# LRU and query products on VectorE, spread x loads, six query tiles, and whole-column expert loads summed in eight shared banks

## The chip, the core and the metric

The kernel runs on one core of a Trainium2 chip. The metric is the device time of one execution in microseconds (us). The core has a matrix engine, TensorE (PE in the profile, with PEld for its weight loads), VectorE (DVE), ScalarE (ACT), GpSimd (POOL) and SyncE (SP, which only issues transfers). Each engine works through its own list of instructions in order and waits where an operand is not ready. SP, ACT and POOL issue DMA transfers. Matrix products accumulate in eight banks of 128 x 512 f32, called `b` in the profile.

## What is computed

One layer of a decoder over 256 tokens of width 2048, with two sub-layers and a modulation (`mod`, from the vector c through `w_ada`):

```python
shift1, scale1, gate1, shift2, scale2, gate2 = split(silu(c) @ w_ada + b_ada, 6)
h = rms_norm(x, norm1_g) * (1 + scale1) + shift1
proj = h @ w_in
lru_out = gelu(lru_gate) * rg_lru(causal_conv(lru_x))     # a recurrence h_t = a_t h_{t-1} + b_t
ssd_out = mamba2_heads(z, xbc, dt)                        # chunked state-space scan
x = x + gate1 * (concat(lru_out, ssd_out) @ w_out)
h2 = rms_norm(x, norm2_g) * (1 + scale2) + shift2
q = h2 @ w_q                                  # 8 heads, product keys, top 16 of 128^2 experts
act = gelu(<h2, u_tab[e]>);  out = sum_k gate_k * act_k * v_tab[e_k]
return rms_norm(x + gate2 * out, final_norm_g)
```

The tables `u_tab` and `v_tab` have 16384 rows of 2048 f32 (134 MB each).

## The kernel before, in words

**Products in two halves.** All large products are f32 made of two parts in the TensorE format: hi = the rounded value, lo = the rest; a product is hi*hi + hi*lo + lo*hi. Weights stream through one pipeline in units of 128 x 1024 f32 (0.5 MB). A unit is loaded into a `raw` buffer (four of them, `NRAW`), ScalarE writes its hi half into an `hl` buffer (L144), VectorE the lo half (L153), TensorE uses it. There are four `hl` buffers (`NHL`), so ScalarE's split of unit n + 4 waits until TensorE is done with unit n. A new load is issued right after a unit's lo, which frees its `raw` buffer. `take` hands a unit to the products, `issue_split` orders the next split, `issue_lo` the lo that lags two splits behind.

**The order.** It is written out by hand: the program emits instructions slot by slot, and side work is put between the slots by `defer` (runs some slots later), `bg_pop` and `bg_flush` (a list of background steps) and `mid` (runs what was deferred). A slot is one unit's products.

**The stages.** Modulation and the first norm (0 to 150 us); input projection with the SSD scan beside it (150 to 434) and the LRU blocks (434 to 555); output projection (555 to 774), whose second half of modulation rows is summed on VectorE: `ada_step` (L384) adds one 128 x 1024 tile of `w_ada`, loaded into one of two `adr` buffers, times a column; the rates `ADA_SSD`, `ADA_LRU`, `ADA_OUT` say how many such steps go with a slot, 96 in all. Then h2 and the query (774 on), then the expert scores.

**LRU.** In `lru_scan` POOL forms gx*m (L694) ahead of the scan, in `lru_out` t*h (L709) behind it, each 128 x 1024, for four blocks.

**h2 and the query.** h2 is made in 16 parts. `h2_t` multiplies x by the inverse norm (VectorE L959, or POOL L957 for odd parts above 2), ScalarE adds the shift and makes hi (L971, or L966 and L967), VectorE makes lo (L969, L973). All parts are ordered ahead of the query products; the loop over four quarters of the columns then takes two units each, for `NQ` = 4 query tiles of 128 outputs (L1211 to L1213), and the other 12 tiles go one by one through `tile_h2` (L444, L446: one 512-wide and one 256-wide matmul per column block).

**Experts.** 80 of the 128 columns of experts (a column is 128 experts) are sparse: all scores are computed (`u_quad`, to 1357 us) and written to memory (`ad`), the chosen ones' weights are gathered back (`w_gather`, L1332, POOL) with the chosen rows of v (`v_gather`, L1323, POOL), and `v_quad` (L1353) sums four tokens at a time: 64 quads, each 32 matmuls. `w_make` prepares a quad's weights: a gelu on ScalarE (L1339), then a product on VectorE into `Wz` (L1343). The other 48 columns (`JD`) are dense: `u_slot` scores all tokens against a column (two half slots per column, 1357 to 1741 us), then `v_slot` (L1439) sums weights times v, twelve matmuls a slot. `wsplit` (L437 on ScalarE, L438 on VectorE) splits one column's weights into hi and lo. `tick` runs after every slot of both dense stretches: it lets the `late` list run (the `w_make` of the next quad) and calls `sparse` when a quad is due.

**Banks and merges.** Quads use banks 0 to 3 for the first 128 tokens and then again for the second; V slots use the other four for the first 1024 output columns over all 48 expert columns, then again for the other 1024. So each set is emptied twice by `merge` (L1461 multiplies by gate 2, L1463 adds to the rows), and the 16 merges lie after quad 31, at the switch of V halves, and at the end. `final` (L1472 to L1483) normalises 128 tokens and stores them.

## Time and profile before

| | |
|---|---|
| median of three runs | 2157.16 us (2155.39 to 2159.13) |
| the profiled execution | 2172.81 us, span 2171.1, mean granted TensorE clock 0.986 |
| TensorE busy | 2089.6 us, 96% of the span, 13092 matmuls |
| VectorE, ScalarE, GpSimd busy | 1397.3, 960.7, 879.2 us |
| moved by DMA | 616.33 MB, mean 284 GB/s |

The profile is of one execution, on one core. Rows of a timeline read: start, length, engine, line, operation, output<-inputs, shapes, count, and in brackets the idle time before with what ended it. The chain of waits follows the last instruction back to what released it, step by step. Groups read: line, engine, operation, shapes, count | busy us, mean ns | idle before and what ended it. "Granted clock" is the share of full speed that TensorE got. Line numbers of the profile of before are those of the listing above; in the changed kernel they are some 5 to 30 higher (L144, L153, L444, L446 become L149, L158, L449, L451; L1353 becomes L1374; L1439, L1450; L437, L442; L1339, L1356; L1343, L1360; L1461 and L1463, L1476 and L1478).

### The profile page before, as it was taken

How to read it: one execution, taken by the hardware profiler on the slowest of the kernel's cores; microseconds unless marked ns; L12 is line 12 of the kernel's file. 1: busy time of each engine (PE TensorE's matmuls, PEld its weight loads, DVE VectorE, ACT ScalarE, POOL GpSimd, SP SyncE). 2: the span in 40 equal slices, each digit the busy share in tenths (PEclk: the TensorE clock that was granted, in tenths of full speed). 3: DMA queues.
4: the chain of work that ended last, by engine and by line, in shares of the span. 5: the costliest groups of instructions: out<-in, count | busy, mean ns of one | idle time of the engine just before them, and what ended most of it. 6: DMA issues, size and time to landing. Idle time of an engine off the chain costs nothing.

```text
span 2171.1 us, 34830 instructions
## 1 busy us (share of the span) xinstructions
PE 2089.6 (96%) x13092; PEld 1639.8 (76%) x13092; DVE 1397.3 (64%) x1996; ACT 960.7 (44%) x1470; POOL 879.2 (40%) x729
## 2 busy tenths in 40 slices
PE   7999999999999989999999999999999989999996
PEld 4779999978999888888788778666666656656663
DVE  2368887978878868879979996334334344344344
ACT  3346665666644454444345554333333333333332
POOL 0013233312212010001415561677777757767774
PEclk9999999999999999999999999999999999999998
DMA  9966566767789954568677778799999999999996
GB/s 372 387 233 223 195 207 216 235 224 251 262 295 322 334 176 166 191 220 282 229 255 238 247 247 288 270 367 346 347 343 354 347 325 346 373 345 348 358 356 234
DMA packets 248264, 616.33 MB, mean 284 GB/s; under 512 B 37752, under 2 KB 121864, under 8 KB 225800
## 3 DMA queue, kind: packets, MB, share of 16 engines
q1 hardware_dynamic: 188944, 387.73, 51.9%
q0 software_dynamic: 45056, 175.52, 21.9%
q10 hardware_dynamic: 14096, 50.86, 6.9%
q8 instruction: 103, 1.69, 0.3%
q14 instruction: 65, 0.53, 0.1%
HBM read 692.41 MB, written 14.69 MB: 326 GB/s over the span
## 4 chain that ended last, share of the span: by engine, by line
PE 70%; DVE 14%; DMA 9%; issue 4%; ACT 2%; POOL 0%; SPq 0%; another core or an unknown queue 0%; DVEq 0%; POOLq 0%; ACTq 0%
PE b L444 13%; PE b L1439 12%; PE b L1353 10%; PE b L446 7%; DVE hl L153 6%; PE b L1281 3%; PE b L1279 3%; PE b L1280 3%; PE b L918 3%; DMA raw<-in_w_in 2%; DMA two<-in_w_ada 2%; DMA adw<-in_w_ada 2%; PE b L812 2%; PE b L813 2%; PE b L814 2%
## 5 line engine op out<-in xcount | busy, mean ns | idle before, releaser
L144 ACT ACTIVATE hl<-raw 128x1024 fp32r<-128x1024 f32 x594 | 628.6, 1060 | 1072.2 <-PE b L1439 192.7
L153 DVE TENSOR_TENSOR hl<-raw,hl 128x1024 fp32r<-128x1024 f32 x594 | 766.5, 1301 | 140.2 <-ACT hl L144 121.0
L444 PE MATMUL b<-H,hl 128*128 128x512 f32 x1376 | 494.2, 402 | 3.2 <-DVE qT L450 2.8
L446 PE MATMUL b<-H,hl 128*128 128x256 f32 x1376 | 386.6, 281 | 5.2 <-DVE hl L153 5.1
L444 PEld LDWEIGHTS b<-H,hl 128*128 128x128 f32 x1376 | 259.1, 188 | 89.9 <-issue 20.2
L1332 POOL DMA_INDIRECT X<-ad,X x256 | 289.5, 1131 | 87.9 <-issue 76.8
L1439 PE MATMUL b<-hl,X 128*128 128x512 f32 x1152 | 279.0, 400 | 11.8 <-issue 10.0
L1439 PEld LDWEIGHTS b<-hl,X 128*128 128x128 f32 x1152 | 216.6, 191 | 87.0 <-issue 39.4
L446 PEld LDWEIGHTS b<-H,hl 128*128 128x128 f32 x1376 | 260.5, 189 | 7.4 <-DVE hl L153 6.6
L1281 PE MATMUL b<-hl,H 128*128 128x512 f32 x640 | 249.9, 390 | 4.0 <-DVE hl L153 3.7
L1279 PE MATMUL b<-hl,H 128*128 128x512 f32 x640 | 252.7, 395 | 0.0
L1280 PE MATMUL b<-hl,H 128*128 128x512 f32 x640 | 249.4, 390 | 0.0
L1323 POOL DMA_INDIRECT vq<-in_v_t,X x128 | 151.5, 1184 | 114.5 <-PE b L1353 38.1
L1323 POOL DMA_INDIRECT tk<-in_v_t,X x128 | 144.0, 1125 | 71.2 <-PE b L1353 31.4
L814 PE MATMUL b<-H,hl 128*128 128x256 f32 x560 | 160.0, 286 | 4.2 <-DVE hl L153 4.2
L1343 DVE TENSOR_TENSOR Wz<-X 128x4 f32<-128x4 f32 x64 | 11.0, 172 | 236.3 <-DMA X<-ad,X 123.0
L812 PE MATMUL b<-H,hl 128*128 128x256 f32 x560 | 162.4, 290 | 0.0
L813 PE MATMUL b<-H,hl 128*128 128x256 f32 x560 | 159.7, 285 | 0.0
L1281 PEld LDWEIGHTS b<-hl,H 128*128 128x128 f32 x640 | 120.1, 188 | 31.7 <-DVE hl L153 6.8
L384 DVE SCALAR_TENSOR_TENSOR adacc<-adr,cact,adacc 128x1024 f32<-128x1024 f32 x90 | 127.7, 1419 | 21.9 <-DMA adr<-in_w_ada 21.8
L1279 PEld LDWEIGHTS b<-hl,H 128*128 128x128 f32 x640 | 120.1, 188 | 23.9
L1280 PEld LDWEIGHTS b<-hl,H 128*128 128x128 f32 x640 | 120.3, 188 | 23.7
(323 smaller groups left out, 3212.2 us busy)
## 6 DMA issues: line engine op xcount, KB each, us to landing
raw<-in_u_t SPq DMA_DIRECT2D x208, 512.0 KB
raw<-in_w_in SPq DMA_DIRECT2D x146, 512.0 KB
adr<-in_w_ada SPq DMA_DIRECT2D x96, 512.0 KB
adw<-in_w_ada SPq DMA_DIRECT2D x64, 512.0 KB
raw<-in_w_o SPq DMA_DIRECT2D x64, 512.0 KB
raw<-in_u_t ACTq DMA_DIRECT2D x48, 512.0 KB
raw<-in_v_t SPq DMA_DIRECT2D x48, 512.0 KB
raw<-in_v_t ACTq DMA_DIRECT2D x48, 512.0 KB
```

Source lines behind the costliest of these rows:

```text
L144: act.activation(t[:, 0], r, AF.Copy)
L153: dve.tensor_sub(t[:, 1], r, t[:, 0].bitcast(FT))
L444: pe.matmul(ps, w[:, 0, c], x[:, k].rearrange("p a b -> p (a b)"), start=(k == 0), stop=False, skip_group_check=True)
L446: pe.matmul(ps[:, :256], w[:, 1, c], x[:, k, 0], start=False, stop=(k == 15), skip_group_check=True)
L812: pe.matmul(ps, wh, hT[:, k, 0, :], start=(k == 0), stop=False)
L1279: pe.matmul(o, hh, w[:, 0, :, kk], start=(k == 0), stop=False)
L1280: pe.matmul(o, hl_, w[:, 0, :, kk], start=False, stop=False)
L1281: pe.matmul(o, hh, w[:, 1, :, kk], start=False, stop=(k == 15))
L1323: pool.indirect_dma_start(x, None, vf, bass.IndirectOffsetOnAxis(ap=eV[:, t:t + 1], axis=0), bounds_check=E1 - 1, oob_is_err=False)
L1332: pool.indirect_dma_start(wA[:, n:n + 1], None, adf, bass.IndirectOffsetOnAxis(ap=eW[:, t:t + 1], axis=0), bounds_check=T * E1 - 1, oob_is ...
L1353: pe.matmul(sb[c][32 * g:32 * g + 32, :], Wz[:, x:x + 32], vs[4 * (q % 2) + g][:, c * 512:(c + 1) * 512], start=(m == 0), stop=(m == 31), ...
L1439: pe.matmul(ob[tb * 2 + c], w[:, i, s], v[:, k, c * 512:(c + 1) * 512], start=(jj == 0 and (i, k) == (0, 0)), stop=(jj == JD - 1 and k == 1))
```

## The change

- **Rates.** `ADA_SSD` .65 to .80, `ADA_LRU` 1.1 to .85, `ADA_OUT` .74 to .80; the number of steps stays 96.
- **POOL to VectorE.** The LRU's two products, and the odd parts of `h2_t`.
- **x loads.** The four loads of x for the second sub-layer's residual go behind output slots 16, 19, 22 and 25 instead of all behind slot 15.
- **Query.** `NQ` = 6. The making of h2 and the query products alternate by quarters: four parts of h2, their products, three splits. In the first quarter the two row copies of x (L855) follow the splits; in the later ones each unit's products stand together.
- **Dense loads.** U and V columns are loaded whole (128 x 2048, 1 MB), alternately from SP and ACT, each into two neighbouring slots of one `raw` tile. V goes column by column, both halves of a column in a row, and `wsplit` runs once per column, the first two in the U slots of columns `JD - 4` and `JD - 3`, the others one column ahead.
- **Shared banks.** `row_bank` gives each (128 tokens, 512 columns) one bank, into which quads and V slots both sum. The merges are left for the end, eight of them.
- **Quads.** The pace is 63 quads over 188 ticks instead of 62 over 192.
- **End.** The last two columns are held back: first 128 tokens of both, quad 61 between, the first four merges, quad 62, then the second 128 tokens, `final(0)`, quad 63, four merges, `final(1)`.

```diff
-ADA_SSD, ADA_LRU, ADA_OUT = 0.65, 1.1, 0.74
+ADA_SSD, ADA_LRU, ADA_OUT = 0.8, 0.85, 0.8
-NQ = 4
+NQ = 6
...
-    items.extend(u_t[J1 + jj][:, h * 1024:(h + 1) * 1024] for jj in range(JD) for h in range(2))
-    items.extend(v_t[J1 + jj][:, h * 1024:(h + 1) * 1024] for h in range(2) for jj in range(JD))
+    items.extend(u_t[J1 + jj] for jj in range(JD))
+    items.extend(v_t[J1 + jj] for jj in range(JD))
...
+    raw = wp.tile([128, NRAW, 1024], FT, name="raw")
     def issue_dma():
...
+        while st["item"] < len(items):
+            n = st["item"]
+            a, w = st["dma"], 1 + (n >= n_alt)
+            if a + w - NRAW > st["lo"]:
+                break
+            o = raw[:, a % NRAW:a % NRAW + w].rearrange("p n c -> p (n c)")
...
-                pool.tensor_tensor(gx, gx, m, op=OP.mult)
+                dve.tensor_tensor(gx, gx, m, op=OP.mult)
...
-            pool.tensor_tensor(t, t, LR["h"], op=OP.mult)
+            dve.tensor_tensor(t, t, LR["h"], op=OP.mult)
...
-            for i in range(4):
-                x_load(i)
+        if n in (16, 19, 22, 25):
+            x_load((n - 16) // 3)
...
-                pool.tensor_tensor(t, x2[k // 4][:, k % 4], rstd2, op=OP.mult)
+                dve.tensor_tensor(t, x2[k // 4][:, k % 4], rstd2, op=OP.mult)
...
+    for q in range(4):
+        w = [take() for _ in range(NQ // 2)] if q == 0 else []
+        for k in range(4 * q, 4 * q + 4):
+            h2_part(k)
+            for e in range(0 if q else NQ):
+                q_mm(w[e // 2], k, e)
+        if q == 0:
+            for _ in range(NQ // 2):
+                issue_split()
+            for f in last:
+                f[1]()
+            continue
+        for n in range(NQ // 2):
+            w = take()
+            for k in range(4 * q, 4 * q + 4):
+                for e in (2 * n, 2 * n + 1):
+                    q_mm(w, k, e)
+            issue_split()
...
+    def row_bank(tb, c):
+        if (tb, c) in sb:
+            return sb[tb, c], False
+        sb[tb, c] = bank(4 * tb + c)
+        return sb[tb, c], True
...
-        if n >= 6 and sq["n"] < 62 * (n - 3) // (4 * JD - 4):
+        if n >= 6 and sq["n"] < 63 * (n - 3) // (4 * JD - 4):
...
-    def v_slot(h, jj):
...
-        if (h, jj) not in Wl:
+    def v_slot(jj, h):
+        if h == 0 and vst["q"] <= jj + 1:
             wsplit()
-        wsplit()
...
-        R[tb, c] = R.get((tb, c), 0) + 1
-        if R[tb, c] == 2:
-            act.activation(ps, a, AF.Square, accum_out=rf[:, tb, c:c + 1])
+        act.activation(ps, a, AF.Square, accum_out=rf[:, tb, c:c + 1])
...
         u_slot(jj)
+        if jj in (JD - 4, JD - 3):
+            wsplit()
...
+    vl = [(jj, h, take()) for jj in (JD - 2, JD - 1) for h in range(2)]
+    issue_lo(0)
+    mid()
+    for tb in range(2):
+        for n, (jj, h, v) in enumerate(vl):
+            v_part(jj, h, tb, v)
+            if tb == 0 and h == 1:
+                if n == 3:
+                    for c in range(4):
+                        merge(0, c, sb[0, c])
+                while late:
+                    late.pop(0)()
+                sparse()
```

How the rows stand, at three places. The first is ScalarE where the query begins: `rstd` is the inverse norm, `H<-adr` and `adr<-adr` make parts of h2 (`H`), `xrow` are the row copies, `hl<-raw` are splits of coming units. Before, its last rows ahead of the splits:

```order
L971 ACTIVATE H<-adr,mod 128x256
L966 ACTIVATE adr<-adr,mod 128x256
L967 ACTIVATE H<-adr 128x256
L855 ACTIVATE xrow<-b_7688 128x512
L855 ACTIVATE xrow<-b_7693 128x512
L144 ACTIVATE hl<-raw 128x1024 x9
```

With the change, from the norm on:

```order
L951 ACTIVATE rstd_7485<-b_6624,epsc 128x256
L975 ACTIVATE H<-adr,mod 128x256 x3
L971 ACTIVATE adr<-adr,mod 128x256
L972 ACTIVATE H<-adr 128x256
L149 ACTIVATE hl<-raw 128x1024 x3
L860 ACTIVATE xrow<-b_7472 128x512
L860 ACTIVATE xrow<-b_7477 128x512
L975 ACTIVATE H<-adr,mod 128x256
L971 ACTIVATE adr<-adr,mod 128x256
```

Part 4 of h2 (the last L975 row) has moved behind three splits and the row copies; the same happens, without the copies, ahead of parts 8 and 12.

The second place is ScalarE at the step from U to V: `xt` is a dense column's scores and their gelu, `X<-Wt` is `wsplit`, the 128 x 4 row is the gelu of a quad's gathered weights. Before:

```order
L136 DMA raw<-in_v_t 128x1024
L449 ACTIVATE xt<-b_16171 128x256
L1339 ACTIVATE X_7791<-X_7791 128x4
L144 ACTIVATE hl<-raw 128x1024
L1409 ACTIVATE xt<-xt 128x256
L449 ACTIVATE xt<-b_16258 128x256
L1409 ACTIVATE xt<-xt 128x256
L437 ACTIVATE X_16316<-Wt 128x256 x2
```

With the change, two columns earlier and at the step:

```order
L1429 ACTIVATE xt<-xt 128x256
L442 ACTIVATE X_15604<-Wt 128x256
L149 ACTIVATE hl<-raw 128x1024
L140 DMA raw<-in_v_t 128x2048
L454 ACTIVATE xt<-b_15607 128x256
L149 ACTIVATE hl<-raw 128x1024
L1429 ACTIVATE xt<-xt 128x256
L1356 ACTIVATE X_7911<-X_7911 128x4
```

The first two `wsplit` rows no longer stand behind the last columns' splits and gelus.

The third place is VectorE at the end: `Wz` is a quad's weights, `b<-b,H` and `H<-H,b` are a merge. Before, the last V slot's merges and what follows:

```order
L1343 TENSOR_TENSOR Wz<-X_7791 128x4
L438 TENSOR_TENSOR X_16316<-Wt,X_16316 128x256 x2
L1461 TENSOR_TENSOR b_17930<-b_17930,H 128x512
L1463 TENSOR_TENSOR H<-H,b_17930 128x512
...
L1343 TENSOR_TENSOR Wz<-X_7791 128x4 x2
L1472 TENSOR_TENSOR H<-H 128x512 x2
```

With the change:

```order
L1360 TENSOR_TENSOR Wz<-X_7911 128x4
L158 TENSOR_TENSOR hl<-raw,hl 128x1024
L443 TENSOR_TENSOR X_15604<-Wt,X_15604 128x256
L158 TENSOR_TENSOR hl<-raw,hl 128x1024
L1476 TENSOR_TENSOR b_12539<-b_12539,H 128x512
L1478 TENSOR_TENSOR H<-H,b_12539 128x512
...
L1360 TENSOR_TENSOR Wz<-X_7911 128x4 x2
L1485 TENSOR_TENSOR H<-H 128x512 x2
```

The weights of quads 62 and 63 stand behind four merges in both; before, the merges were of the V banks and a quad followed them at once, now they are of the first 128 tokens, and 24 more V matmuls follow quad 62.

More of the change, by code (lines that the diff above doesn't have):

```diff
@@ L334, in hybrid_kernel @@
         if n == 2:
-            for _ in range(NRAW):
-                issue_dma()
+            issue_dma()
         mid()
@@ L960, in h2_t, with h2_part @@
                                          op0=OP.mult, op1=OP.mult)
[L961 to L963 removed]
+    pq = [bank(1 + n) for n in range(NQ // 2)]
+    def h2_part(k):
         t = ht[k // 4][:, k % 4]
@@ L971, in hybrid_kernel, with q_mm @@
             act.activation(h2[:, k, 0], t, AF.Identity, bias=mod[:, 4, k:k + 1])
-            h2_t(k + 2)
             dve.scalar_tensor_tensor(h2[:, k, 1], t, mod[:, 4, k:k + 1], h2[:, k, 0].bitcast(FT),
                                      op0=OP.add, op1=OP.subtract)
-    for f in last:
-        f[1]()
+        h2_t(k + 2)
+    def q_mm(w, k, e):
+        ps = pq[e // 2][:, (e % 2) * 256:(e % 2) * 256 + 256]
+        c = slice((e % 2) * 512 + k % 4 * 128, (e % 2) * 512 + (k % 4 + 1) * 128)
+        first = k == 0 and e % 2 == 0
+        pe.matmul(ps, w[:, 0, c], h2[:, k, 0], start=first, stop=False, skip_group_check=True)
+        pe.matmul(ps, w[:, 0, c], h2[:, k, 1], start=False, stop=False, skip_group_check=True)
+        pe.matmul(ps, w[:, 1, c], h2[:, k, 0], start=False, stop=(k == 15), skip_group_check=True)
+    h2_t(0)
+    h2_t(1)
+    for q in range(4):
[16 more added lines that the diff above has]
+            issue_split()
     mixs.close()
@@ L1516, in hybrid_kernel @@
     mid()
-    for h in range(2):
-        for jj in range(JD):
-            v_slot(h, jj)
-            if h == 0 and jj in (0, JD // 2, JD - 4):
-                rows_load((0, JD // 2, JD - 4).index(jj))
+    for jj in range(JD - 2):
+        for h in range(2):
+            v_slot(jj, h)
+            if h == 0 and jj in (0, JD // 3, 2 * JD // 3):
+                rows_load((0, JD // 3, 2 * JD // 3).index(jj))
             tick()
-    while sq["n"] < 63:
-        tick()
-        sparse()
-    tick()
+    assert sq["n"] == 61
+    wsplit()
+    vl = [(jj, h, take()) for jj in (JD - 2, JD - 1) for h in range(2)]
+    issue_lo(0)
     mid()
-    mid()
+    for tb in range(2):
+        for n, (jj, h, v) in enumerate(vl):
+            v_part(jj, h, tb, v)
+            if tb == 0 and h == 1:
[5 more added lines that the diff above has]
+                sparse()
+    while late:
+        late.pop(0)()
     final(0)
```

84 lines of the change are left out of this document (28 added, 56 removed).

## Prediction

> **What bounds the kernel now.** I read the page's busy line first, then the engines stretch by stretch (columns: stretch, its length, busy time with instruction count of PE, PEld, DVE, ACT, POOL, then granted clock, DMA share, GB/s).
> ```profile
> PE 2089.6 (96%) x13092; PEld 1639.8 (76%) x13092; DVE 1397.3 (64%) x1996; ACT 960.7 (44%) x1470; POOL 879.2 (40%) x729
> 150.00:434.00 284.00, 279.16 (x2081) 259.13 (x2081) 244.41 (x340) 171.00 (x314) 91.86 (x79) 1.00 0.64 211
> 434.00:555.00 121.00, 112.73 (x724) 102.58 (x722) 95.89 (x103) 82.67 (x117) 25.34 (x14) 0.97 0.71 235
> 555.00:774.00 219.00, 212.55 (x1491) 199.29 (x1490) 175.10 (x175) 103.29 (x127) 31.91 (x21) 0.98 0.86 301
> 1357.00:1737.00 380.00, 377.49 (x2426) 254.22 (x2425) 146.55 (x214) 128.63 (x215) 285.51 (x242) 1.00 0.93 339
> 1737.00:2147.00 410.00, 395.80 (x2200) 250.15 (x2198) 168.75 (x248) 137.37 (x235) 283.55 (x260) 0.98 0.95 345
> ```
> TensorE is the bound at 96%, and the change removes no sizable TensorE work. What can be won are its holes: 8 us in the LRU stretch, 6 in the output projection, 14 in the dense V stretch, and the clock lost behind them. The dense U stretch has 2.5 us of holes in 380. Two numbers price a V stretch: three slots of twelve matmuls, and one sparse quad, at full clock.
> ```profile
> 2126.10 3.57 PE b L1353 x32
> 2129.67 8.38 PE b L1439 x36
> ```
> So a slot is 8.38/3 = 2.79 us, and a slot with its third of a quad 2.79 + 3.57/3 = 3.98.
>
> **Dense V, gains.** At the step from U to V, `wsplit` (L437) stood behind a split that waited for a transfer, and TensorE stood still (a timeline: start, length, idle before).
> ```profile
> 1744.58 1.06 ACT L144 ACTIVATE hl<-raw 128x1024 fp32r<-128x1024 f32 x1 [3.64 <-remote]
> 1747.54 5.49 PE L1439 MATMUL b<-hl,X 128*128 128x512 f32 x12 [6.41 <-issue]
> ```
> The first two `wsplit`s now come three and two U columns before the end; the V units themselves were split ahead. Gone: 6.41, and 5.49 - 2.79 = 2.70 of slow clock, together 9.1 (0 if the late transfer holds the slot anyway; three units lie ready, so I take 9.1). At the switch of halves, merges on VectorE freed the banks in pieces:
> ```profile
> 1946.81 3.01 PE L1439 MATMUL b<-hl,X 128*128 128x512 f32 x12
> 1957.89 2.35 PE L1353 MATMUL b<-tk,Wz 128*32 128x512 f32 x20
> ```
> 11.08 us for three slots instead of 8.38; there is no switch any more: 2.7. Twice the ScalarE `wsplit` stood behind a gelu that waited for gathered weights:
> ```profile
> 1898.54 0.20 ACT L1339 ACTIVATE X<-X 128x4 f32<-128x4 f32 x1 [2.85 <-DMA X<-ad,X]
> 1899.10 4.61 PE L1439 MATMUL b<-hl,X 128*128 128x512 f32 x12 [1.80 <-issue]
> 1926.70 4.61 PE L1439 MATMUL b<-hl,X 128*128 128x512 f32 x12 [1.79 <-ACT X L437]
> ```
> Each cost 1.8 + (4.61 - 2.79) = 3.6. A `wsplit` now serves two slots and runs two slots ahead, so a 2.85 us delay is covered by 5.6; but splits still queue behind the gelu. I take 5 of 7.2 (ends 0 and 7.2).
> The last two rows also tell about the clock: an idle gap of 1.8 us was followed by a slot at 4.61 instead of 2.79. [...]
>
> **Dense loads, whole columns.** 96 loads of 1 MB replace 192 of 0.5 MB, each into two of four slots, so a load is issued when both slots are free. For 0.5 MB the nearest landings and ScalarE's waits are
> ```profile
> 45.63 10.76 DMA raw<-in_w_in
> 555.96 5.06 DMA raw<-in_w_o
> ACT hl L144 <- DMA raw<-in_u_t: 84.4, 48, 4.2
> L153 DVE TENSOR_TENSOR hl<-raw,hl 128x1024 fp32r<-128x1024 f32 x594 | 766.5, 1301 | 140.2 <-ACT hl L144 121.0
> 1382.53 6.29 PE L1353 MATMUL b<-vq,Wz 128*32 128x512 f32 x32 [1.15 <-issue]
> ```
> The loop of a pair of slots is four slots of TensorE, 4 x 3.98 = 15.9; less two splits of 1.06 (the row at 1744.58) and one lo of 1.30 (L153's mean), a load may take 12.5. Twice 5.06 is 10.1, twice 10.76 is 21.5, but that one lay behind a full queue with four loads at once; here at most two are under way. I take 1.5 us of loss for single late loads (0 to 24, the first rival). [...] `wsplit` falls from 96 to 48 on ScalarE and VectorE, which idle there: nothing.
>
> **First quad.** It is gated by the gathers of its weights, and moves forward by one half slot (8 pairs of matmuls, 0.35 us each):
> ```profile
> 1362.13 1.00 POOL L1332 DMA_INDIRECT X<-ad,X  x1 [10.12 <-DMA raw<-in_u_t]
> 1367.21 0.40 PE L444 MATMUL b<-H,hl 128*128 128x512 f32 x1
> 1367.56 0.40 PE L444 MATMUL b<-H,hl 128*128 128x512 f32 x1
> 1368.91 3.64 PE L1353 MATMUL b<-tk,Wz 128*32 128x512 f32 x32 [0.84 <-issue]
> ```
> The gathers start no earlier, so TensorE waits 2.8 longer: loss 2.8 (0 to 5 with slow clock).
>
> **Output projection.** Four x loads went in at once and delayed the `w_ada` transfer, on which an accumulation (L384) and behind it a lo waited:
> ```profile
> 630.27 11.73 DMA adr<-in_w_ada
> 644.58 0.58 PE L874 MATMUL b<-ylru,hl 128*128 128x256 f32 x1 [3.76 <-DVE hl L153]
> 650.49 0.21 PE b L873
> 653.12 0.12 PE b L873
> ```
> The matmuls of the six microseconds behind it took 0.21 each where 0.12 is usual: some 3 us more. Three slots apart, I take a gain of 4.5 (1 to 7). The rate .80 adds 2.5 `w_ada` steps at 1.42 (L384's mean, below) and 1.2 MB in a stretch with DMA at .86: loss 1 (0 to 3).
>
> **LRU and SSD.** Eight products leave POOL for VectorE, four of L694 and four as large of L709.
> ```profile
> L694 POOL TENSOR_TENSOR X<-X,X 128x1024 f32<-128x1024 f32 x4 | 10.9, 2724 | 57.2 <-ACT X L693 57.2
> L384 DVE SCALAR_TENSOR_TENSOR adacc<-adr,cact,adacc 128x1024 f32<-128x1024 f32 x90 | 127.7, 1419 | 21.9 <-DMA adr<-in_w_ada 21.8
> 502.68 4.62 DVE L384 SCALAR_TENSOR_TENSOR adacc<-adr,cact,adacc 128x1024 f32<-128x1024 f32 x2
> ```
> VectorE has no such row; the nearest is L153 at 1.30, so 8 x 1.3 = 10.4 us more. Against that, beside a POOL product two accumulations took 4.62 instead of 2.84, so eight products cost VectorE up to 8 x 1.8 = 14 already, and the rate .85 takes about 7 steps of 1.42 = 10 away. VectorE comes out some 10 us lighter, of which holes and slow clock (8.3, and 0.03 x 121 = 3.6) can return 10 at most; that a product is done 1.4 sooner helps as well. I take a gain of 5 (-4 to 10: the lower end if POOL's work was hidden). In the SSD stretch 4.6 more steps load VectorE by 6.6, where it is 244 of 284 busy: loss 1.5 (0 to 4).
> [...]
>
> **Query.** TensorE's rows and ScalarE's at the place:
> ```profile
> 776.80 2.78 DVE L959 SCALAR_TENSOR_TENSOR adr<-X,mod,rstd 128x256 f32<-128x256 f32 x3
> 778.44 0.58 PE L1211 MATMUL b<-H,hl 128*128 128x256 f32 x1 [3.98 <-ACT H L971]
> 780.02 0.58 PE L1212 MATMUL b<-H,hl 128*128 128x256 f32 x1 [1.00 <-DVE H L973]
> 790.09 1.07 ACT L855 ACTIVATE xrow<-b 128x512 f32<-128x512 f32 x2
> 791.05 3.90 ACT L144 ACTIVATE hl<-raw 128x1024 fp32r<-128x1024 f32 x4
> ```
> Before, ScalarE produced all sixteen hi parts ahead of any split, so TensorE never waited after 780. Now part 4 stands behind three splits and two row copies, and the first of these splits needs the buffer that TensorE reads until its last step of the first quarter: 3 x 0.98 + 1.07 + 0.5 (a hi, taken as one of the two row copies) less 12 matmuls of 0.12 still running, 3.1, with the semaphores 3.5, plus 1.9 of slow clock: 5.4. At the second and third quarter one split (0.98) and one hi (0.5) lie behind TensorE's end, with lo and semaphores 2.1 each. Gained: without POOL's product the three rows at 776.80 need about 1.1 instead of 2.78, and the 1.00 gap shrinks by 0.6: 2.3. Two more tiles as three matmuls instead of a wide pair: 0.2. Net loss 5.4 + 4.2 - 2.3 + 0.2 = 7.5 (3 to 13).
>
> **Tail.**
> ```profile
> 2148.57 5.34 PE L1353 MATMUL b<-tk,Wz 128*32 128x512 f32 x32 [4.00 <-DVE Wz L1343]
> 2160.54 0.69 DVE H L1463
> 2161.23 0.62 DVE b L1461
> ```
> Before, quad 62 waited 4.0 for its weights, and the second half's merges stood behind the first half's finish. Now quad 62's weights (L1360) stand behind four merges (two operations each, 4 x (0.69 + 0.62) and steps between), so TensorE waits about 5.2 there, then has 24 matmuls and quad 63 to do, and the last merges follow without the finish between. Laid out row by row the end comes 1.4 earlier (-5 to 2 later).
>
> **Sum.** Gains 9.1 + 2.7 + 5 + 2 + 4.5 + 5 + 1.4 = 29.7; losses 1.5 + 2.8 + 1 + 1.5 + 7.5 = 14.3; net 15.4. The profiled execution took 2172.81 (span 2171.1), 0.7% over the median of 2157.16, with no stretch that stands out; I take 15.4 off both: 2157.4 for such an execution, 2142 for the median.
>
> **Rivals.** (1) Slower: two 1 MB loads in the ring are too few. From a landing of 12.5 us each further 1 us costs one per loop, 48 loops: at 13.0 it is 24 us, 2142 + 24 = 2166; it outweighs the gain from 12.8. For it: 84.4 us of ScalarE waits for 0.5 MB loads already, DMA at .93 to .95. Against: only 10.1 by the row at 555.96, and TensorE's 2.5 us of holes in 380. 0.11. (2) No change: the dense stretches are limited by DMA, and what TensorE wins there is given back as waits for loads; then only 4.5 + 5 + 1.4 - 1 - 1.5 - 7.5 = 0.9 is left: 2156. For it: .95. Against it this row of the page, slices of 54 us:
> ```profile
> GB/s 372 387 233 223 195 207 216 235 224 251 262 295 322 334 176 166 191 220 282 229 255 238 247 247 288 270 367 346 347 343 354 347 325 346 373 345 348 358 356 234
> ```
> 372 and 387 were reached, 345 is the V stretch. 0.12. [...] (3) The VectorE moves don't do what they say: LRU at -4 and the query at 13, 2142 + 9 + 5.5 = 2157. 0.07. The forecast, 0.70: 2124 (stalls, LRU and x loads at their upper ends, 2.2 + 5 + 5 + 2.5 more, and 3.5 less lost in the query) to 2152.
>
> The measurement tells a change from 0.2%, 4.3 us, on. Faster: the forecast and a little of rival 3, 0.72; same: rival 2 and most of 3, 0.15; slower: rival 1 and a worse tail or query, 0.13. Range 2124 to 2160: it leaves out rival 1's long end and the best sums.
>
> **What would show it.** No idle before the first V slot, none in mid V; TensorE holes of some 3.5, 2 and 2 us among the query products at granted clock under 1; a wait of about 3.6 before the first quad and 5 before quad 62; LRU holes halved; L384 without doubled rows; ScalarE's wait for `raw` in the dense stretches not above 84 us. Wrong I am if loads land after 12.5 us, or if the query holes are wider than computed.

## The result: 1.2% slower

The changed kernel took 2180.28 us (median of five, 2176.14 to 2189.18) beside 2155.39 of the kernel before: a ratio of 1.0118, 95% interval 1.01 to 1.0137. Forecast was 2142, and faster. The page of the changed kernel looks as before, which is why busy shares don't help here:

```profile
PE 2096.2 (96%) x13124; PEld 1648.5 (75%) x13124; DVE 1361.1 (62%) x1945; ACT 945.9 (43%) x1422; POOL 873.7 (40%) x714
```

VectorE, ScalarE and GpSimd do less, TensorE is at 96% again. So the two programs are compared stage by stage, each stage ending where a given matmul starts or ends in the timeline. "Before" is the execution that the prediction was made from (2172.81 us), "before again" a second profile of the same kernel (2153.51 us, close to the median), "changed" an execution of 2189.18 us.

| stage, us | before | before again | changed | changed less before again |
|---|---|---|---|---|
| input projection, SSD | 289.9 | 289.9 | 295.6 | +5.7 |
| input projection, LRU | 136.7 | 135.0 | 135.7 | +0.7 |
| output projection, first half | 102.2 | 102.9 | 98.7 | -4.2 |
| output projection, second half | 98.5 | 98.5 | 101.2 | +2.7 |
| norm's sum to first score unit (query) | 105.8 | 105.8 | 114.7 | +8.9 |
| scores of the sparse columns | 467.6 | 468.9 | 473.7 | +4.8 |
| to the first quad | 21.5 | 21.4 | 22.0 | +0.6 |
| first quad to the end of U | 371.9 | 363.6 | 379.3 | +15.7 |
| V to the end | 430.3 | 418.3 | 419.0 | +0.7 |

The border between the first two rows lies at slot 42 of the input projection, and the LRU row ends at 573 us, where the first matmul of the output projection starts. The rate of modulation steps changes from `ADA_SSD` to `ADA_LRU` ten slots ahead of that border, at slot 32.

Two things are seen at once. Up to the first quad a stage of unchanged code mostly repeats within 3 us from profile to profile (`best_c` and `best_d` below, which are the same up to there, differ by 4.1 in one), and 19 us were lost there. And the first profile of before was no typical execution in its last two stages: 20 us of its time there are missing in the second. For those two stages single profiles say little. Five profiles with the old order give 790 us from the first quad to the end on average (367 and 423), seven with the new order and 1 MB loads 796 (374 and 422). So of the 25 us that the medians differ by, 19 lie ahead of the first quad and about 6 behind it.

The longest waits of TensorE in the changed kernel (us in total, times, longest), each of which comes up below; the row left out, 7.9 us in the modulation, has its like in `b0` with 7.7:

```profile
PE b L1374 <- DVE Wz L1360: 10.0, 4, 5.0
PE b L984 <- ACT H L975: 9.5, 4, 3.4
...
PE b L449 <- DVE Wz L1360: 7.0, 2, 3.9
PE b L398 <- DVE ggt L455: 5.0, 1, 5.0
```

### The profile page after: what moved, and what is told of

The parts are those of the page before. It is cut to its first block, busy times and chain, and to the rows that moved or that the text cites. A ratio compares the mean times of both kernels' runs of the same rounds, so it can differ in the third digit from the quotient of the medians.

```text
span 2187.1 us, 34476 instructions
## 1 busy us (share of the span) xinstructions
PE 2096.2 (96%) x13124; PEld 1648.5 (75%) x13124; DVE 1361.1 (62%) x1945; ACT 945.9 (43%) x1422; POOL 873.7 (40%) x714
## 4 chain that ended last, share of the span: by engine, by line
PE 61%; DMA 18%; DVE 9%; issue 6%; ACT 3%; POOL 2%; SPq 0%; DVEq 0%; POOLq 0%; ACTq 0%
PE b L449 9%; PE b L1450 8%; PE b L1374 7%; PE b L1296 5%; PE b L1298 5%; PE b L1297 5%; PE b L451 5%; DMA adw<-in_w_ada 4%; DVE hl L158 4%; DMA tk<-in_v_t,X 4%; DMA vq<-in_v_t,X 3%; PE b L817 2%; DMA adr<-in_w_ada 2%; PE b L818 2%; PE b L819 2%
## 5 line engine op out<-in xcount | busy, mean ns | idle before, releaser
L449 PE MATMUL b<-H,hl 128*128 128x512 f32 x1344 | 489.1, 406 | 9.4 <-DVE Wz L1360 7.0
L451 PE MATMUL b<-H,hl 128*128 128x256 f32 x1344 | 379.9, 283 | 2.4 <-DVE hl L158 2.4
L1349 POOL DMA_INDIRECT X<-ad,X x256 | 302.8, 1183 | 86.6 <-issue 81.7
L449 PEld LDWEIGHTS b<-H,hl 128*128 128x128 f32 x1344 | 255.6, 190 | 97.7 <-issue 33.2
L1450 PE MATMUL b<-hl,X 128*128 128x512 f32 x1152 | 271.0, 393 | 0.0
L451 PEld LDWEIGHTS b<-H,hl 128*128 128x128 f32 x1344 | 256.8, 191 | 3.4 <-DVE hl L158 3.1
L1340 POOL DMA_INDIRECT tk<-in_v_t,X x128 | 150.5, 1176 | 52.6 <-issue 30.1
L817 PE MATMUL b<-H,hl 128*128 128x256 f32 x560 | 161.8, 289 | 2.1 <-DVE mod L402 2.1
L819 PE MATMUL b<-H,hl 128*128 128x256 f32 x560 | 159.1, 284 | 1.3 <-DVE hl L158 1.3
L818 PE MATMUL b<-H,hl 128*128 128x256 f32 x560 | 159.1, 284 | 0.0
L389 DVE SCALAR_TENSOR_TENSOR adacc<-adr,cact,adacc 128x1024 f32<-128x1024 f32 x90 | 117.7, 1307 | 26.3 <-DMA adr<-in_w_ada 25.7
## 6 DMA issues: line engine op xcount, KB each, us to landing
adw<-in_w_ada SPq DMA_DIRECT2D x64, 512.0 KB, 10.8
```

What stands on the lines that cost most here:

```text
L449: pe.matmul(ps, w[:, 0, c], x[:, k].rearrange("p a b -> p (a b)"), start=(k == 0), stop=False, skip_group_check=True)
L451: pe.matmul(ps[:, :256], w[:, 1, c], x[:, k, 0], start=False, stop=(k == 15), skip_group_check=True)
L817: pe.matmul(ps, wh, hT[:, k, 0, :], start=(k == 0), stop=False)
L818: pe.matmul(ps, wh, hT[:, k, 1, :], start=False, stop=False)
L1340: pool.indirect_dma_start(x, None, vf, bass.IndirectOffsetOnAxis(ap=eV[:, t:t + 1], axis=0), bounds_check=E1 - 1, oob_is_err=False)
L1349: pool.indirect_dma_start(wA[:, n:n + 1], None, adf, bass.IndirectOffsetOnAxis(ap=eW[:, t:t + 1], axis=0), bounds_check=T * E1 - 1, oob_is ...
```

## The experiments

They ran on more than one chip; the kernel before took 2155 to 2156 us beside some of them and 2165 beside others. So each result is the ratio to the kernel before, run beside it on the same chip; the changed kernel's is 1.0118. Stage times are each from one profile.

### Which stalls were real

`b0`: the kernel before, unchanged.

> The kernel before, unchanged, for a second profile of it. The execution profiled first took 2172.81 us, the median of five is 2155.39. Theory 1: the 17 us between them are the stalls in the dense V stretch that the prediction took as gains (6.4 us before the first V slot, two slots of 4.61, merges at the switch), and they come and go from execution to execution: a profile of an execution near the median shows few of them, and the V stretch with the tail (430.3 us from the end of U to the end) is 10 to 17 us shorter. Rival: those stalls are fixed by the order of the program and are there again, within 2 us; the 17 us lie elsewhere or are spread evenly.

0.9993 (0.9982 to 1.0004). Theory 1 held. In the execution near the median the hole ahead of the first V slot is 3.0 us and the slot behind it took 3.04 (2.79 at full clock), where 6.4 and 2.7 had been priced:

```profile
1736.86 3.12 PE L1439 MATMUL b<-hl,X 128*128 128x512 f32 x12 [3.03 <-ACT X L437]
1739.90 3.64 PE L1353 MATMUL b<-tk,Wz 128*32 128x512 f32 x32
```

No slot of 4.61 follows a gap in V (the one slot as long, 4.69, is the switch of halves with its merges), and no quad in U takes over 3.7, where ten took 3.8 to 6.3 in the first profile.

### The query

`no_query`: the query stage of before put back whole (`NQ = 4`, h2 made ahead, its odd products on POOL).

> The changed kernel with the query stage of before: four query tiles, h2 made whole ahead of the products, odd parts on POOL. Between the norm's sum and the first sparse score unit the changed kernel took 114.7 us, before 105.8, and the score stretch behind it 473.9 against 467.9. Theory 1: both are the query stage's (TensorE stands behind splits there, and the top-k work starts later): 12 to 15 us less than the changed kernel, 2165 to 2168. Rival: only the local 9 us come back, 2171. Rival 2: the order of the query stage doesn't matter and the loss is the DMA's: 2177 to 2181.

1.0056 (1.0037 to 1.0076), some 13 us less. The two stages read 105.8 and 468.1, as before (105.8, and 467.6 and 468.9): theory 1. Two more runs split the edit.

`six_ahead`: six tiles, but h2 made whole ahead of the products.

```diff
-    for q in range(4):
-        ... h2_part(k) for this quarter, its products, three splits ...
+    for k in range(16):
+        h2_part(k)
+    for f in last:
+        f[1]()
+    for q in range(4):
+        ... products of six tiles, three splits ...
```

> The changed kernel with its six query tiles, but all sixteen parts of h2 made ahead of the products and splits, as before the change. The changed kernel spent 114.7 us from the norm's sum to the first score unit (105.8 with the old query stage) and 473.7 on the scores (468.1). Theory 1: the 9 us are the order's, because parts of h2 stand behind splits on ScalarE; they go: 105 to 107, and 2170 in all. What of the scores' 5 us comes from six tiles instead of four stays. Rival: the six tiles themselves delay the top-k work; both stages stay within 2 us of the changed kernel, 2178 to 2181.

`four_inter`: `NQ = 4`, interleaved as in the change.

> The changed kernel with four query tiles, interleaved with the making of h2 as changed. Theory 1: the first stage stays 7 to 10 us too long (113 to 116 instead of 105.8), since the splits still stand ahead of parts 4, 8 and 12, and each quarter's products are now shorter (two units instead of three) and cover less; the score stretch is back at 468 if the six tiles were its cause. In all 2172 to 2177. Rival: the first stage falls to 106 to 108, because it was the six tiles.

`six_ahead` 1.0118 (1.0102 to 1.0135), `four_inter` 1.0077 (1.0053 to 1.0101). The query stage took 114.0 in the one and 115.2 in the other; either edit alone costs the whole 9 us, and both together no more. The theory for `six_ahead` was wrong; its rival's numbers came out, but the rival's reason, the top-k work, says nothing of the 9 us. The theory for `four_inter` held. ScalarE's timelines tell why. In the changed kernel the splits wait for TensorE to finish the first quarter, and part 4 of h2 comes behind them and the row copies:

```profile
791.53 2.95 ACT L149 ACTIVATE hl<-raw 128x1024 fp32r<-128x1024 f32 x3 [6.58 <-PE b L986]
794.38 1.06 ACT L860 ACTIVATE xrow<-b 128x512 f32<-128x512 f32 x2
795.34 0.50 ACT L975 ACTIVATE H<-adr,mod 128x256 fp32r<-128x256 f32 x1
```

In `six_ahead` ScalarE makes h2 until 794, and only then splits; TensorE, done with the first quarter at 791.8, waits for a split instead of a part:

```profile
794.19 1.07 ACT L860 ACTIVATE xrow<-b 128x512 f32<-128x512 f32 x2
795.15 2.95 ACT L149 ACTIVATE hl<-raw 128x1024 fp32r<-128x1024 f32 x3
```
```profile
PE b L984 <- ACT hl L149: 4.4, 1, 4.4
```

A quarter of six tiles uses three of the four `hl` buffers, so only one unit of the next quarter can be ready: the wait comes after 78 matmuls, the 72 of the first quarter and 6 more. A quarter of four tiles uses two, and two are ready. The score stretch's 4.8 us are the six tiles': 472.5 with six, 468.7 with four. Why six cost them there was not tried.

### The rates and the LRU

`old_rates`: .65, 1.1, .74 in the changed kernel.

> The changed kernel with the three rates of before (.65, 1.1, .74). In the changed kernel's profile the SSD stretch took 295.8 us against 290.2, with 3 us more of holes and 2 of slow clock, the LRU stretch 0.9 less than before, the second half of the output projection 2.8 more. Theory 1: the rate .80 loads VectorE in the SSD stretch and the rate .80 the output projection: 5 to 8 us less than the changed kernel, 2172 to 2175, unless the LRU stretch takes 3 us of it back. Rival: the rates are a wash, the 5.6 us of the SSD stretch come from run to run: 2178 to 2182.

1.0056 (1.004 to 1.0073): 13 us less, more than theory 1 had. SSD 289.9, LRU 135.2, output projection 95.1 and 98.5 instead of 98.7 and 101.2. VectorE's load alone did not explain that, and `best_b`, below, speaks against it: with 15 steps instead of 20 up to slot 32 (rate .5) the SSD stretch took 299.5, longer still. The timelines of both show a wait at L398, the eight column sums that finish a group of 16 steps:

```profile
453.83 3.54 PE L398 MATMUL b<-ones,adacc 128*128 128x1 f32 x16 [5.04 <-DVE ggt L455]
```
```profile
390.22 0.99 PE L398 MATMUL b<-ones,adacc 128*128 128x1 f32 x4 [6.21 <-DVE xct L426]
```

The first is the changed kernel, the second `best_b`. Up to slot 43 a finish goes into the bank of the tile before, which VectorE must have emptied; and there VectorE waited for ScalarE, which was loading tables and working on the scan (the changed kernel):

```profile
447.09 1.28 ACT L621 ACT_TABLE_LOAD   x1
...
448.87 1.28 ACT L691 ACT_TABLE_LOAD   x1
450.16 1.70 ACT L691 ACTIVATE X<-X,lspn 128x256 f32<-128x256 f32 x4
451.90 1.06 ACT L692 ACTIVATE X<-X 128x1024 f32<-128x1024 f32 x1
452.86 0.37 ACT L454 ACTIVATE ggt<-b 128x256 f32<-128x256 f32 x1
```
```profile
453.26 0.42 DVE L455 TENSOR_TENSOR ggt<-b,ggt 128x256 f32<-128x256 f32 x1 [7.44 <-ACT ggt L454]
```

Counting steps by the rates, the finishes fall on slots 27 and 44 before, 22 and 42 changed, 34 and 46 in `best_b`. Slot 44 is the first at which a finish has bank 6 to itself.

`fin_bank`: one number of the changed kernel.

```diff
-        ada["bank"] = 6 if slot >= 44 else (slot + 2) % 3
+        ada["bank"] = 6 if slot >= 42 else (slot + 2) % 3
```

> The changed kernel with one number: from slot 42 on instead of 44 the finish of a modulation group (eight column sums on TensorE) goes into bank 6 and not into the bank of the tile before. In the changed kernel the second group's finish falls on slot 42, and TensorE waited 5.0 us for VectorE to empty that bank (before, it fell on slot 44, with bank 6). Theory 1 (the rates cost time through where the finishes fall): the 5 us and the slow clock behind go, the LRU stretch falls from 135.7 to 127 to 130. Rival (the wait only shows that VectorE is late, and the next tile waits instead): 134 to 136.

The LRU stretch fell to 128.7 (from 135.7), the hole is gone; 1.0098 (1.0081 to 1.0115). Theory 1 held: 7 of that stretch's us lay in one misplaced finish (the whole got some 4 shorter). The SSD stretch was not tried by itself, but the starts of its slots in the traces tell where its 5.7 us went. Against `b0` the changed kernel loses 1.2 in slots 16 to 18, 6.3 in slots 22 and 23, where its finish stands, and gains 1.8 in slot 27, where the finish of before stood; every other slot is equal within 0.1, with 24 steps instead of 20. `best_b` loses 11.8 in slots 34 and 35, where its finish stands, gains the same 1.8, and is equal within 0.3 elsewhere. So 4.5 of the 5.7 go by where the finish stands, and the load of four more steps shows nowhere else. At slot 22 the wait itself is short,

```profile
PE b L398 <- DVE X L455: 1.2, 1, 1.2
```

but the granted clock from 306 to 315 us, behind it, was 0.62.

In the output projection the rates cost in another way too. With .80 TensorE's waits for lo on VectorE come to 3.4 us there, with the old rates to 0.2, which is theory 1 of `old_rates`; and a finish moved from slot 59 to 61, the first slot of this stretch, which took 2.6 longer.

`pool_products`: the LRU's two products back on POOL in the changed kernel.

> The changed kernel with the two LRU products back on POOL. The LRU stretch took 135.0 us before (rate 1.1, POOL), 135.7 changed (.85, VectorE), 135.2 with the old rates and VectorE. Theory 1: neither the products' engine nor the rate is on the path there, the stretch stays at 134.5 to 136.5, and the whole at 2178 to 2182. Rival, the prediction's: VectorE products save 5: the stretch gets 4 to 6 longer, 2184 to 2186.

1.0123 (1.0097 to 1.0148). The LRU stretch took 131.2 instead of 135.7, the half behind it 100.2 instead of 98.7: both expectations missed; by these stages POOL is 3 us better, by the whole it is not. VectorE's price was as forecast, and the accumulations did get quicker (mean 1425 in `b0`, 1370 in this run, 1307 changed), rows of the changed kernel:

```profile
L699 DVE TENSOR_TENSOR X<-X,X 128x1024 f32<-128x1024 f32 x4 | 4.9, 1226 | 5.3 <-ACT X L698 5.2
L714 DVE TENSOR_TENSOR ggt<-ggt,X 128x1024 f32<-128x1024 f32 x4 | 4.9, 1225 | 1.0 <-ACT ggt L713 0.7
L389 DVE SCALAR_TENSOR_TENSOR adacc<-adr,cact,adacc 128x1024 f32<-128x1024 f32 x90 | 117.7, 1307 | 26.3 <-DMA adr<-in_w_ada 25.7
```

But L699 now waits 5.2 us on VectorE for ScalarE's root, with lo and accumulations queued behind it; on POOL they did not. Its longest wait (4.4) comes 12 us behind the misplaced finish, and a finish's sum queued behind it holds TensorE for 2.1. In `fin_bank` L699 waits 0.8 in all, and with the old rates the engine made no difference (135.2 on VectorE, 135.0 on POOL). So the products' price seems to hang on the misplaced finish; a run with both products on POOL and the finish in bank 6 was not made.

`x_loads`: the kernel before with spread x loads alone.

> The kernel before with the four x loads apart, nothing else. The first half of the output projection took 102.9 us before, 98.7 changed, 95.1 changed with the old rates. Theory 1: spreading the loads is worth 7 to 8 us there (95 to 96), 2147 to 2149 in all. Rival: the prediction's 4.5 us, 2151; the rest of the 7.8 came from the LRU products, whose end lies in this stretch.

0.998 (0.9964 to 0.9995): faster. The first half of the output projection took 97.4 instead of 102.9, between theory and rival.

### The dense stretches

`half_loads`: 0.5 MB loads in the new order.

> The changed kernel with 0.5 MB loads in the dense stretches, each half column into one slot, in the new order of columns; all else as changed. Theory 1: large loads cost the dense stretches something, since quads there wait for gathered rows and weights more often than before (in V nine quads over 3.7 us against two): 5 to 10 us less than the changed kernel, 2170 to 2175. Rival, the first of the prediction: the 1 MB loads are the main loss: 2155 to 2165. Rival, the forecast's: large loads relieve the gathers, and the kernel gets 1 to 5 slower, 2181 to 2185.

1.0084 (1.0066 to 1.0101): 7 us less, theory 1's size, against the forecast's sign. `best_a` and `best_b` with the same loads took 800 and 794 from the first quad to the end, no less than with 1 MB loads (796). But they ran where the kernel before takes 2165, and that excess seems to lie mostly behind the first quad (`x_loads`, run there, came to it at 1367.0 us, `b0`, beside 2155, at 1369.9), so the size is not settled. Medians from issue to landing, in the dense stretches of the changed kernel and of `b0`:

```profile
raw<-in_v_t SPq DMA_DIRECT2D x24, 1024.0 KB, 8.8
...
tk<-in_v_t,X POOLq DMA_INDIRECT x120, 9.4
```
```profile
raw<-in_v_t SPq DMA_DIRECT2D x48, 512.0 KB, 7.3
...
tk<-in_v_t,X POOLq DMA_INDIRECT x120, 8.4
```

8.8 us is below the 12.5 at which rival 1 began, and the gathers got a little slower, not faster (9.4 beside 8.4). But the median hides late loads. ScalarE's waits for columns of U and V, in the changed kernel and in `half_loads`, which has none for V:

```profile
ACT hl L149 <- DMA raw<-in_v_t: 128.5, 24, 8.6
ACT hl L149 <- DMA raw<-in_u_t: 112.4, 42, 9.4
```
```profile
ACT hl L149 <- DMA raw<-in_u_t: 65.3, 35, 6.5
```

Most of these waits cost TensorE nothing. Two did: the work that stood behind such a split on ScalarE and VectorE came late, a quad's weights last, and TensorE stood still. These are the 7.0 us of L449 in the list of waits:

```profile
1500.51 1.06 ACT L149 ACTIVATE hl<-raw 128x1024 fp32r<-128x1024 f32 x1 [9.43 <-DMA raw<-in_u_t]
1502.44 0.53 PE L449 MATMUL b<-H,hl 128*128 128x512 f32 x1 [3.90 <-DVE Wz L1360]
```
```profile
1751.15 1.06 ACT L149 ACTIVATE hl<-raw 128x1024 fp32r<-128x1024 f32 x1 [8.59 <-DMA raw<-in_u_t]
1753.08 0.47 PE L449 MATMUL b<-H,hl 128*128 128x512 f32 x1 [3.06 <-DVE Wz L1360]
```

The two loads had landed 11.4 and 10.8 us after their issue, so 12.5 was too much to allow. In the other profiles with the new order, 1 MB loads and all gathers, such waits of L449 in the dense stretches come to 0.2 to 4.8 us, in `half_loads` to none. Rival 1 happened, but small.

The gathers come late as well, and quads wait for them even in the middle of V:

```profile
1805.33 1.06 PE L1374 MATMUL b<-vq,Wz 128*32 128x512 f32 x6
1807.32 3.62 PE L1374 MATMUL b<-vq,Wz 128*32 128x512 f32 x26 [0.93 <-DMA vq<-in_v_t,X]
```

Ten of V's quads took 3.8 to 5.6 us there instead of 3.6, 10 us in all; in `b0` one did. Four runs ask what limits the transfers; each computes only part of the sum, as its expectation says.

`less_gather`: `if q >= 64 or (q >= 2 and g >= 2): return` in `v_gather` of the changed kernel.

> The changed kernel without half of the gathered rows of v: from the third quad on only two of a quad's four tokens get new rows (the other two reuse old ones), so about 60 MB and 124 indirect transfers less in the dense stretches; every matmul stays. Theory 1 (the dense stretches are at the DMA's limit, and the holes that the change closed come back as late weights and late rows): the late quads and the stalls vanish, U falls from 379 to 362 to 366 and V with the tail from 419 to 410 to 413, all of it at a DMA share under .85; about 18 to 24 less than the changed kernel on the same chip. Rival (the late weights come from the order of the queue on POOL, ScalarE and VectorE): POOL has fewer issues too, but the stalls of U and the first-quad wait of 4.4 stay; less than 8 us gained.

`half_rows`: gathers of `x[:, :1024]` from rows half as long.

> The changed kernel with every gathered row of v half as long (1024 columns into the first half of the row's tile, the other half reused), as many indirect transfers on POOL as before, but 64 MB less. Theory DMA (the dense stretches are at the DMA's limit of .92 to .95): the late quads and stalls vanish as they did with half the gathers, 18 to 23 less than the changed kernel. Theory POOL (eight issues of at least 1.3 us per quad are 10.4 of the 12 us between quads; POOL's queue is the limit): less than 8 gained, late quads stay.

`few_w`: `if n % 4 > 1: return` in `w_gather`.

> The changed kernel with half of the weight gathers left out (two of a quad's four; the other weights stay zero), all rows of v gathered: 128 fewer transfers on POOL of 128 values each, under 0.1 MB less. Theory POOL: with six issues per quad instead of eight POOL runs ahead, late quads and stalls vanish, 18 to 23 less than the changed kernel. Theory DMA: under 8 gained, since the bytes stay.

`old_less_gather`: the edit of `less_gather` in the kernel before.

> The kernel before with the same half of the gathered rows left out as in the run with half the rows (two of four tokens), for what the new order of the dense stretches is worth where gathers are no limit: from the first quad to the end the changed kernel took 778.6 us with half the rows. Theory 1 (the changed order closes 10 to 15 us of holes, wherever gathers keep up): the old order takes 788 to 794, and the whole is only 0 to 4 less than the kernel before, whose order leaves the gathers their time. Rival (the new order is worth nothing in itself): 776 to 782.

| | ratio (interval) | first quad to end of U | V to the end |
|---|---|---|---|
| new order, mean of seven | | 374 | 422 |
| `less_gather` | 1.0015 (1.0004 to 1.0026) | 369.6 | 409.0 |
| `half_rows` | 1.007 (1.0053 to 1.0086) | 368.4 | 411.1 |
| `few_w` | 1.0066 (1.0046 to 1.0087) | 373.6 | 412.6 |
| old order, mean of five | | 367 | 423 |
| `old_less_gather` | 0.9973 (0.9962 to 0.9984) | 363.9 | 413.3 |

The windows over U and V of the changed kernel, `half_rows` and `few_w` (stretch, length, busy PE, PEld, DVE, ACT, POOL, clock, DMA share, GB/s):

```profile
1389.00:1768.00 379.00, 371.42 (x2399) 249.75 (x2396) 144.02 (x213) 125.16 (x212) 287.47 (x241) 0.99 0.92 339
1768.00:2165.00 397.00, 388.63 (x2175) 244.30 (x2177) 139.32 (x183) 119.56 (x182) 297.25 (x257) 0.99 0.95 355
```
```profile
1388.00:1757.00 369.00, 368.86 (x2404) 248.84 (x2408) 145.06 (x214) 124.59 (x213) 290.84 (x243) 1.00 0.72 239
1757.00:2141.00 384.00, 377.99 (x2156) 239.46 (x2152) 139.93 (x183) 119.84 (x182) 305.04 (x254) 1.00 0.75 249
```
```profile
1389.00:1763.00 374.00, 369.66 (x2400) 248.28 (x2400) 143.71 (x214) 124.50 (x213) 200.97 (x180) 1.00 0.92 343
1763.00:2150.00 387.00, 380.84 (x2162) 241.58 (x2164) 142.17 (x187) 120.48 (x185) 211.52 (x191) 1.00 0.95 363
```

With half the bytes and every issue (POOL stays at 291 and 305 us) the stretches fall to the floor of `less_gather` within 1 us in sum, and from the second quad to the last but two no late load or row holds TensorE any more (one wait of 1.0 for weights is left), so bytes are a limit. (`less_gather` had V as expected, and U some 4 above its 362 to 366.) Fewer issues at the same bytes also help, and by ratio as much: `half_rows` gained some 10 us, where its DMA theory had 18 to 23, and `few_w` 11, where the same theory had under 8. The stages of `few_w` are from its slowest execution (2177, its median is 2172). So issues, or their small packets (23632 under 512 B in the changed kernel from 1390 to 2140 us, with 482 indirect issues), have a part as well, and the split between the two stays open. (The ratio of `less_gather` is probably flattered: it ran where the kernel before takes 2165, yet took 2168 where `half_rows`, run where it takes 2156, took 2171.) The two floors answer the other question: 778.6 in the new order, 777.2 in the old (788 to 794 expected). The new order is worth nothing by itself: V is 4.3 shorter, U 5.7 longer. Of these 5.7, 2.8 are the half slot that now lies behind the first quad, and the rest can be that quad's slow clock: it took 6.6 in `less_gather`, after a wait of 3.6, and 3.6 in `old_less_gather`, after one of 0.6. (In the changed kernel it waited 4.2 and took 5.9.) And from its floor to its average execution the new order loses 18 us to late transfers, the old order 13.

The V stretch's rate, changed and with fewer issues, is 355 and 363 GB/s, at a DMA share of .95 in both.

`late_first`: at the end the weights of quad 62 ahead of the merges.

```diff
+                while late:
+                    late.pop(0)()
                 if n == 3:
                     for c in range(4):
                         merge(0, c, sb[0, c])
-                while late:
-                    late.pop(0)()
```

> The changed kernel with one swap at the end: the weights of quad 62 are made ahead of the four merges of the first 128 tokens, not behind them. TensorE waited 5.1 us ahead of quad 62 and had slow clock for some 2 us after. Theory 1: that wait is on the path to the end, since 24 matmuls, quad 63, merges and the store follow; it goes, and the stretch from the end of V to the end gets 4 to 7 shorter. Rival: the gathered weights of quad 62 land late anyway (5.1 us from issue to landing in the profile of before), and the gain is under 2.

Ahead of quad 62, the changed kernel and then this one:

```profile
2160.92 5.58 PE L1374 MATMUL b<-tk,Wz 128*32 128x512 f32 x32 [4.97 <-DVE Wz L1360]
```
```profile
2151.93 1.06 PE L1374 MATMUL b<-tk,Wz 128*32 128x512 f32 x6 [2.24 <-DVE Wz L1360]
2153.79 5.32 PE L1374 MATMUL b<-tk,Wz 128*32 128x512 f32 x26 [0.80 <-issue]
```

3.0 us of waits instead of 5.0, so the wait itself gives 2, nearer the rival. The ratio 1.0052 (1.0035 to 1.0068) claims 14; that much cannot come from this place, and I put no more than the 2 down to it.

### Versions that should beat both

`best_a`: the changed kernel with old rates, old query, POOL products, 0.5 MB loads.

> What the runs so far leave: the changed kernel with the old rates, the old query stage, LRU products on POOL and 0.5 MB loads, so the kernel before plus spread x loads, column order in V, shared banks, one weight split per column, the new pace and end. By stages: 290 for SSD, 135 LRU, 95 to 97 and 98.5 for the output projection, 105.8 and 468.5, as before but for 6 to 7 us in the output projection; in the dense stretches theory 1 (the V changes close 7 to 11 us of holes and lose about as much to late gathers and a longer wait at the end) gives 0 to 5 more. In all 0.3 to 0.5% faster than before. Rival: the V changes are worth the 11 us of holes that the second profile of before still showed, 0.8% faster.

`best_b`: the same with rates .5, 1.35, .74 and the edit of `late_first`.

> The same with two more edits: modulation steps moved out of the SSD stretch into the LRU stretch (rates .5, 1.35, .74), and the weights of quad 62 ahead of the merges. Theory 1 (4.65 steps cost 5.7 us in the SSD stretch, where VectorE sets the pace, and seven steps less freed 4 in the LRU stretch): SSD 284 to 286, LRU 138 to 140, so 1 us gained by the rates, and 4 to 7 at the end; 0.6 to 0.8% faster than before. Rival: below the rate .65 VectorE no longer sets SSD's pace, SSD stays at 289 to 290 and the LRU stretch loses 4: the rates cost 3 us.

`best_c`: the kernel before with the spread x loads and rates .65, .9, .83.

> The kernel before with the spread x loads and the rates .65, .9, .83. By these rates the finishes of the modulation groups fall on slots 27 and 47 of the input projection, as 27 and 44 before, so none waits for a tile's bank; five to six steps move from the LRU stretch to the output projection. Theory (rates cost through where the finishes fall, and the LRU stretch gains from fewer steps): SSD 290, LRU 129 to 132 instead of 135.0, output projection 96 to 98 and 98.5 to 101 instead of 102.9 and 98.5; 0.3 to 0.5% faster than before. Rival: steps cost as much in the output projection as they save in the LRU stretch: 0.2% faster, the x loads alone.

`best_d`: the same, with one `wsplit` at U column `JD - 3`.

> The same, with the weights of the first V slot split three U columns before the end. The second profile of before still showed a hole at the step from U to V (11.9 us instead of 8.5 for the 44 matmuls around it). Theory: 2 to 4 us less than the run without this edit, where the hole shows. Rival: the gathers are the limit of the dense stretches and take the 3 us back: within 1 us of it.

`best_a` 0.9998 (0.9988 to 1.0008): no better than the x loads without the new order, and both expectations missed. `best_b` 1.0064 (1.0047 to 1.0081): its rival was half right (LRU 139, 4 longer), its theory wrong; SSD 299.5 with the finish on slot 34. `best_c` 1.0007 (0.9996 to 1.0019) missed both as well: the good slots kept SSD at 289.9, but LRU came to 136.8 and the second half of the output projection to 105.2, where finishes now wait for the last accumulation:

```profile
PE b L393 <- DVE adacc L384: 3.1, 2, 2.5
```

`best_d` 0.9986 (0.9975 to 0.9996), by the ratio some 4 us better than `best_c`, the size of its theory. But its profile is 4.3 us ahead at the first quad already, where the two programs are the same (LRU 132.6 and 101.7 for 136.8 and 105.2), and takes 784 us from there against 782. The wait of 3.0 ahead of the first V slot became 0.7, and one of 2.5 came ahead of the fourth. So a gain from closing the hole is not shown. The only edit that makes the kernel before faster is the x loads, by 0.2%; `best_d` contains it.

## Why the prediction was wrong

Term by term, gains positive; "shown" is from the stages and runs above.

| term | forecast | shown |
|---|---|---|
| hole at U to V, two late V slots, late quads | +9.1 +5 +2 | mostly one execution's; given back (late quads of V -10) |
| switch of halves | +2.7 | gone, inside the +4.3 of V |
| first quad earlier | -2.8 | -5.7, with the slow clock behind the wait |
| 1 MB loads | -1.5 | 0 to -7, not settled; two waits of 7.0 in the changed kernel |
| x loads | +4.5 | +5.5 by itself |
| output rate | -1 | -3.6 and -2.7 in the two halves |
| SSD rate | -1.5 | -5.7 |
| LRU | +5 | -0.7: rate +3.8 with the finish's -7 in it, products -4.5 |
| query | -7.5 | -8.9, and -4.8 in the scores |
| end | +1.4 | wait 5.0 as computed (5.2), inside the +4.3 |

**The failed step of the sum** is the one sentence that takes 15.4 "off both" executions because the profiled one had "no stretch that stands out". It stood out: the 17 us over the median were the dense stretches' stalls, and 16.1 us of the gains (9.1, 5 and 2) were those same stalls, of which the second profile shows little more than the hole of 3.0. Taken off a median execution the rest can't be had; without it the forecast's own terms sum to 15.4 - 13.1, some 2 us, no change. The 25 us of loss come from the other terms: the query, the rates, the loads and the first quad.

**What bounds the dense stretch.** With holes gone from TensorE's order, gathers and loads come late instead; that is rival 2 of the prediction, held at 0.12. It was held low by the 387 GB/s of a slice at the start, before the gathers begin, against which 345 looked far from a limit. Of rival 1 a small part happened: the largest landing was 11.4 us, under the 12.5 that were allowed, and yet TensorE stood still, because the allowance left out the work that queues behind a split. The prediction's own sign for it, no more than 84 us of ScalarE's waits for `raw` in the dense stretches, failed: they came to 193. Most of the loss came without it. The sum's 2 us for late quads (the one at 1382.53 had lost 6.29 - 3.57 = 2.7) no run shows: with 1 MB loads the gathers took 9.4 us from issue to landing beside 8.4 in `b0`, and ten of V's quads came late where one did there.

**The rates** were the second failed step, and the largest that no rival covered: priced as VectorE load (steps times 1.42), they also move the points at which a group is finished on TensorE, into a bank that is another tile's. The listing of `ada_step` and `pe_due` tells where they fall; I counted the steps and not the slots. In the output projection the load counts as well (3.4 us of waits for lo), where 1 was forecast.

**LRU.** The price of a product (1.3 forecast, 1.226 measured) and the relief of the accumulations were right; that a product which waits for ScalarE holds up VectorE's queue was left out. In `fin_bank` that wait is nearly gone, so its price hangs on the finish too.

**Query, right in mechanism.** Holes of 3.5, 2.1 and 2.1 were forecast, and the changed kernel has waits of 9.5 in four: 3.4 that was there in the first place (4.0 before), then 3.0, 1.5 and 1.5. That is the sum without what it allowed for semaphores and lo; slow clock behind a second hole (0.83 from 808 to 818 us) was not in it. What was left out are the scores behind two fewer background tiles, 4.8 us; that it is their top-k work is likely and not shown. That six tiles alone would cost as much, by the buffers, was not seen either.

## What to carry to other kernels

Before a stall in a profile is booked as a gain, check how far the profiled execution lies from the median: if it is slower by about the sum of those stalls, they are that execution's and not the program's. Here indirect gathers and large loads together kept the DMA at a share of .92 to .95, and closing holes on the matrix engine moved the wait to the transfers (18 us between the floor and the average execution); halving the bytes in one run showed the floor. A median time to landing says little of the few late loads that stop the matrix engine (8.8 us here, where the two that stopped it took 11.4 and 10.8); the longest waits behind them do. A rate that spreads side work over slots also decides on which slot its rarer steps fall, and one such step on a bank still in use cost 7 us of the LRU stretch here.

## What was not expected of the hardware

In the first profile gaps of 1.8 us were followed by a slot of slow clock (4.61 instead of 2.79; granted clock 0.66 from 1899 to 1904 and 0.72 from 1926 to 1932), but in `b0` the gap of 3.03 us was not: from the start of its twelve matmuls to the quad are 1739.90 - 1736.86 = 3.04 us. In the changed kernel the gap of 3.06 at 1753 was followed by a granted clock of 1.00, the one of 3.90 at 1502 by 0.59 over 4 us. So the length of a gap alone doesn't tell its price, and a sum should carry both.
